# A hybrid encoder layer in float32: x normalised and split once more during the token-major projection, all neighbourhood-attention weights turned by VectorE and DMA, and attention values moved half a step on

## The chip, the cores and the metric

The kernel runs on one core of a Trainium2 chip. The metric is the device time of one execution in microseconds (us). Engines are named as the profile names them: PE is TensorE (matmuls), PEld its weight loads, DVE VectorE, ACT ScalarE, POOL GpSimd, SP the queue from which most DMAs are issued. Three timed runs of the kernel before gave 872.6 to 873.25 us, median 873.25.

## The reference

One layer over 512 tokens with 1024 channels, all float32. `h` is the RMS norm of `x`, and one wide projection feeds everything:

```python
h = rms_norm(x, mix_norm_g[l])
proj = h @ w_in[l]
ml_q, ml_k, ml_v, ml_o, ml_gates, na_qkv, xa_q, merge_pre = jnp.split(proj, split_points, axis=-1)
y_ml = mlstm_branch(ml_q, ml_k, ml_v, ml_o, ml_gates, ...)        # bidirectional, 4 heads of 128
y_na = neighbourhood_attention(na_q, na_k, na_v, na_rpb[l])       # 8 heads of 64, 8 x 64 token grid
y_xa = memory_cross_attention(xa_q, mem_k, mem_v)                 # 4 heads of 128, 256 memory tokens
gates = jax.nn.sigmoid((merge_pre + b_merge_gate[l]).astype(F32)).astype(x.dtype)
merged = g_ml * (y_ml @ w_br_ml[l]) + g_na * (y_na @ w_br_na[l]) + g_xa * (y_xa @ w_br_xa[l])
x = x + merged @ w_out[l]
x = x + conv_glu_ffn(rms_norm(x, ffn_norm_g[l]), w_ffn_up[l], ...)
return rms_norm(x, final_norm_g)
```

The norm scales each token by one number, so it can be applied to `x` before a projection or to the projection's result after it. In the neighbourhood attention each query attends to a window of 8 rows by 16 columns; the softmax weights are then multiplied with the values, for which they must lie with the keys on the partitions, that is, transposed.

## The kernel before, in words

**Precision.** PE multiplies in a reduced float32 format, so each float32 operand is split into a high and a low part, and each product is three matmuls (`mm3`, lines 222, 223, 224: high x high, high x low, low x high). Weights arrive by DMA in blocks of mostly 512 KB (`emit_raw`), up to three blocks ahead, and each is split one block ahead of its use: an ACT copy makes the high part (line 204), a VectorE subtraction the low part (line 205).

**Stages.** `XH`, `XL` are the split of x times its gain, but not yet times the norm of each token. With them run the projections of mLSTM q and k (`mlq`, `mlk`); the *token-major part* (`TMW`, blocks `tm`, three groups of columns in eight weight blocks), in which x is the stationary operand and tokens come out on partitions, for the mLSTM and neighbourhood values; then, channels on partitions again, `xaq`, `o`, memory keys and values, `naq`, `nak`; and three branches (`br` 0 to 2), each with eight gate projections (`g`) and four blocks of branch projection (`br`), followed by the output projection and the FFN. Every projection on `XH`, `XL` comes out of PSUM through a product with the token's norm: `rc` per partition in the token-major part, `rb` along the row elsewhere (VectorE, lines 1037, 1045, 1081, 1086 and, for the gates, 1109; the gates and `o` then go through a tanh on ACT).

**The attentions beside it.** The mixers (`ml_all`, `xa_all`, `na_all`) are generators. The projections call `step` or `half` in their midst, and each call runs the current generator up to its next `yield`, so that attention instructions are interleaved with projections; a gate projection drives two half steps of the neighbourhood attention, and a branch projection of one output tile one. The place of an instruction in its engine's queue then comes from the framework's own scheduling of what the generators emit. `drain` runs what is left before a branch projection reads its mixer's output.

**Neighbourhood attention.** 16 tiles (4 head pairs x 2 heads x 2 halves). In step t `scores` makes four matmuls (lines 817, 818) and the softmax of tile t. Then the weights must be turned. Tiles below `TN` = 8: `transposes`, four PE transposes into PSUM (line 836), split from there (lines 843, 844). Tiles from 8: `turn_out`, a VectorE transpose of 32 x 32 blocks (line 142) and four strided DMAs to DRAM (`td`, line 145), one step later `turn_in`, one DMA back (line 151), and `parts`, the split (lines 854, 855). `values` multiplies (line 866), `store` collects heads and splits the result (lines 882 to 889). For tiles from 8 the values stand in the second half of step t + 2. The values' right operand is loaded by 32 small POOL DMAs for each head pair (`load_vwin`, line 497).

**Memory attention.** `xa_all` works head by head with the same turning; its values stood one yield after the split of its weights.

Of the kernel before, what the change touches and what calls it, by code (L numbers as in the profile page):

```python
# [17 lines left out]
P = 128  # L18
S = 512
# [8 lines left out]
NU = 14  # L28
EB = 6
WARM = 15  # L30
TN = 8
RM, RB = 0.65, 1.3
EPS = 1e-6
NEG = -1e30
# [69 lines left out]
def hybrid_block(ctx, tc, xT, memT, wflat, vecs, gbias, nabias, outa, outb):  # L104
# [14 lines left out]
    def nm(s):  # L119
        uid[0] += 1  # L120
        return f"{s}_{uid[0]}"
# [13 lines left out]
    def atps():  # L135
        return atp.tile([P, 512], F32, tag="at", name=nm("at"))
# [17 lines left out]
    def by4(a):  # L154
        return a.rearrange("p (s b) -> p s b", s=4)
# [301 lines left out]
    def to_nav(c, t, src):  # L457
# [319 lines left out]
    def na_all(nq, nk, vw0, yh, yl):  # L777
# [52 lines left out]
                A.activation(smv[:, j, :], smv[:, j, :], AF.Copy, scale=su[:, j:j + 1])  # L830
            return sm

        def transposes(i, sm):
            pt = atps()
            for j in range(4):
                PE.transpose(pt[:, j * P:(j + 1) * P], sm[:, j * P:(j + 1) * P], ident)  # L836

            pp = []
            for bl in range(2):
                w = tp.tile([P, 4, P], F32R, tag="E", name=nm("w"), bufs=EB).rearrange("p a b -> p (a b)")  # L840
                wv = w.rearrange("p (k x q) -> p k x q", k=2, x=2)
                src = pt[:, bl * 256:(bl + 1) * 256].rearrange("p (k q) -> p k q", k=2)
                A.activation(wv[:, :, 0, :], src, AF.Copy)
                V.tensor_tensor(wv[:, :, 1, :], src, wv[:, :, 0, :].bitcast(F32), op=ALU.subtract)
                pp.append(w)
            return pp

        def parts(u):
            pp = []
            for bl in range(2):  # L850
# [40 lines left out]
        n = 16  # L891
        ops = prep(0)
        bt = bias_tile(0)
        sms, ds, us, pts = {}, {}, {}, {}
        vws = {0: vw0}

        def out(i):
            if i % 4 == 0 and i + 4 < n:
                vws[i // 4 + 1] = load_vwin(i // 4 + 1)
            store(i, values(i, pts.pop(i), vws[i // 4]))  # L900

        yield
        yield
        for t in range(n + 2):
            if t < n:
                nb = bias_tile(t + 1) if t + 1 < n else None
                sms[t] = scores(t, ops, bt)
                bt = nb
                if t % 4 == 3 and t + 1 < n:
                    ops = prep((t + 1) // 4)  # L910
            if t - 2 in us:
                pts[t - 2] = parts(us.pop(t - 2))
            elif t - 2 in pts:
                out(t - 2)
            if t - 1 in ds:
                us[t - 1] = turn_in(ds.pop(t - 1), "E", EB)
            yield
            if t - 1 in sms:
                pts[t - 1] = transposes(t - 1, sms.pop(t - 1))
            if TN <= t < n:  # L920
                ds[t] = turn_out(by4(sms.pop(t)))
            if t - 2 >= TN:
                out(t - 2)
            yield


    def xa_all(xq, mk, mv, yh, yl):
# [53 lines left out]

        q, k = prep(0)
        yield
        yield
        u = None
        for h in range(5):
            if u:
                pT = parts(u)
            if h < 4:
                sm = [scores(tq, q, k) for tq in range(2)]  # L990
            yield
            if u:
                values(h - 1, v, pT)
            if h == 4:
                break
            ds = [turn_out(by4(x)) for x in sm]
            yield
            u = [turn_in(d, "E", EB) for d in ds]
            yield
            v = prep_v(h)  # L1000
            if h < 3:
                q, k = prep(h + 1)
            yield
        yield


    gens = []
# [25 lines left out]

    xq = unit()
    for f in range(4):
        ps = proj(("xaq", f), XH, XL, at=mid())
        V.tensor_tensor(xq[:, f * S:(f + 1) * S], ps, rb, op=ALU.mult)
        mem_part(f)
        step(RB / 2)
    for f in range(4):  # L1040
        if f == 2:
            mp = rstd_parts(macc, M)
        ps = proj(("o", f), XH, XL, at=mid({4: lambda: norm.append(rstd_cols(mp, M, "m"))} if f == 3 else {}))
        t = scr()
# [4 lines left out]
        A.activation(g.rearrange("p (i s a) -> p s i a", i=4, s=4), t.rearrange("p (s i a) -> p s i a", s=4, i=4),  # L1049
                     AF.Tanh, scale=0.5)  # L1050
        V.tensor_scalar(g, g, 1.0, None, op0=ALU.add)
        step(RB / 2)
# [24 lines left out]
    nq, nk = unit(), unit()  # L1077
    rv = lambda a: a.rearrange("p (r b c) -> p b r c", r=ROWS, b=4)
    for f in range(4):
        ps = proj(("naq", f), XH, XL, at=mid())  # L1080
        V.tensor_tensor(nq[:, f * S:(f + 1) * S].rearrange("p (b r c) -> p b r c", r=ROWS, b=4), rv(ps), rv(rb),
                        op=ALU.mult)
        step(RB / 2)
    for f in range(4):
        ps = proj(("nak", f), XH, XL, at=mid())
        V.scalar_tensor_tensor(nk[:, f * S:(f + 1) * S], ps, 0.125, rb, op0=ALU.mult, op1=ALU.mult)
        step(RB / 2)

    mg = []
# [8 lines left out]
    for br in range(3):  # L1098
# [6 lines left out]
            ys[2] = [unit(F32R), unit(F32R)]  # L1105
            gens.append(na_all(nq, nk, vw0, *ys[2]))
        def gate(f, t):
            ps = proj(("g", br, f), XH, XL, at={3: half, KT - 1: half})
            V.tensor_tensor(t, ps, rb, op=ALU.mult)
# [329 lines left out]
```

## Time and profile before

| what | value |
|---|---|
| timed runs (3) | 872.6 to 873.25 us, median 873.25 |
| the profiled execution's own time | 872.36 us |
| its span, first to last instruction | 870.6 us |
| mean granted TensorE clock | 0.998 |
| DMA issues of weight turning before (all uses) | 112 writes `td<-s`, 28 reads `U<-td` |
| gate products with the norm (line 1109) | 24, 0.68 us each |

In the page, section 1 gives busy time and its share of the span, section 4 the chain of work that ended last. Groups of instructions read: line, engine, operation, output<-input, shape, count, then busy time and mean ns, then idle time ahead of them and who ended it. In a timeline the columns are start, duration, engine, line, operation. Bars on PE overlap, since a matmul's duration includes the pipeline behind it: how much of PE a matmul takes is read from the distance between starts.

### The profile page before, as it was taken

How to read it: one execution, taken by the hardware profiler on the slowest of the kernel's cores; microseconds unless marked ns; L12 is line 12 of the kernel's file. 1: busy time of each engine (PE TensorE's matmuls, PEld its weight loads, DVE VectorE, ACT ScalarE, POOL GpSimd, SP SyncE). 2: the span in 40 equal slices, each digit the busy share in tenths (PEclk: the TensorE clock that was granted, in tenths of full speed). 3: DMA queues.
4: the chain of work that ended last, by engine and by line, in shares of the span. 5: the costliest groups of instructions: out<-in, count | busy, mean ns of one | idle time of the engine just before them, and what ended most of it. 6: DMA issues, size and time to landing. Idle time of an engine off the chain costs nothing.

```text
span 870.6 us, 12197 instructions
## 1 busy us (share of the span) xinstructions
PE 862.5 (99%) x4214; PEld 727.2 (84%) x4214; DVE 596.1 (68%) x1200; ACT 447.6 (51%) x937; POOL 137.4 (16%) x218
## 2 busy tenths in 40 slices
PE   9999999999999999999999999999999999999997
PEld 7898889988888888888888888888888888888896
DVE  7696688876568768898676568777633466667443
ACT  7464457764355657787634445444422344444442
POOL 1001100000104810751001112111100011111010
PEclk9999999999999999999999999999999999999999
DMA  8235654642445733576523332223223322322443
GB/s 276 97 100 157 183 177 139 195 133 97 133 140 151 226 113 119 152 203 218 182 91 107 129 118 88 97 98 106 86 85 114 110 99 95 102 94 74 142 119 110
DMA packets 59598, 114.37 MB, mean 131 GB/s; under 512 B 8200, under 2 KB 30216, under 8 KB 59536
## 3 DMA queue, kind: packets, MB, share of 16 engines
q1 hardware_dynamic: 51888, 107.14, 38.0%
q0 software_dynamic: 7360, 6.32, 3.4%
q8 instruction: 33, 0.54, 0.3%
q14 instruction: 29, 0.24, 0.1%
q10 hardware_dynamic: 288, 0.14, 0.1%
HBM read 102.01 MB, written 11.55 MB: 130 GB/s over the span
## 4 chain that ended last, share of the span: by engine, by line
PE 98%; issue 0%; DMA 0%; DVE 0%; ACT 0%; POOLq 0%; POOL 0%; DVEq 0%; ACTq 0%
PE mm L223 29%; PE mm L222 29%; PE mm L224 29%; PE at L222 2%; PE at L223 2%; PE at L224 2%; PE at L866 1%; PE at L684 1%; PE at L686 1%; PE at L668 1%; PE at L817 0%; PE at L818 0%; PE at L628 0%; PE at L836 0%; DMA vec<-vecs 0%
## 5 line engine op out<-in xcount | busy, mean ns | idle before, releaser
L222 PE MATMUL mm<-u,w 128*128 128x512 f32 (+1 forms) x1077 | 416.4, 387 | 0.1
L223 PE MATMUL mm<-u,w 128*128 128x512 f32 (+1 forms) x1077 | 413.8, 384 | 0.3 <-DVE u L229 0.3
L224 PE MATMUL mm<-u,w 128*128 128x512 f32 (+1 forms) x1077 | 414.0, 384 | 0.0
L204 ACT ACTIVATE w<-wr 128x512 fp32r<-128x512 f32 (+1 forms) x298 | 184.6, 622 | 207.7 <-PE mm L224 171.6
L205 DVE TENSOR_TENSOR w<-wr,w 128x512 fp32r<-128x512 f32 (+3 forms) x299 | 208.2, 699 | 89.0 <-ACT w L204 86.5
L224 PEld LDWEIGHTS mm<-u,w 128*128 128x128 f32 x1077 | 202.3, 188 | 41.1 <-DVE w L205 0.6
L222 PEld LDWEIGHTS mm<-u,w 128*128 128x128 f32 x1077 | 202.5, 188 | 38.8 <-ACT u L228 0.4
L223 PEld LDWEIGHTS mm<-u,w 128*128 128x128 f32 x1077 | 202.5, 188 | 38.7 <-DVE u L229 0.6
L497 POOL DMA_DIRECT2D u<-nav_d x128 | 62.6, 516 | 97.6 <-PE at L866 50.9
L1309 POOL TENSOR_TENSOR s<-s,rb 128x512 f32<-128x512 f32 x22 | 37.3, 1697 | 248.6 <-DVE s L1308 240.6
L228 ACT ACTIVATE u<-s 128x512 fp32r<-128x512 f32 x22 | 13.9, 632 | 56.2 <-DVE s L1312 56.2
L1312 DVE TENSOR_TENSOR s<-mm,s 128x512 f32<-128x512 f32 x22 | 15.2, 690 | 22.5 <-POOL s L1309 22.5
L409 ACT ACTIVATE s<-pad,vec 128x512 f32<-128x512 f32 x30 | 24.4, 813 | 8.6 <-DVE pad L407 8.1
L410 DVE SCALAR_TENSOR_TENSOR s<-pad,vec,s 128x512 f32<-128x512 f32 x30 | 23.5, 783 | 4.6 <-ACT s L409 4.6
L1159 POOL TENSOR_TENSOR acc<-acc,s 128x512 f32<-128x512 f32 x7 | 9.0, 1289 | 102.8 <-ACT s L1158 102.8
L229 DVE SCALAR_TENSOR_TENSOR u<-s,u 128x512 fp32r<-128x512 f32 x22 | 15.2, 691 | 14.0 <-ACT u L228 14.0
L1308 DVE SCALAR_TENSOR_TENSOR s<-s,s 128x512 f32<-128x512 f32 x22 | 15.2, 692 | 13.4 <-ACT s L1307 13.3
L411 DVE SCALAR_TENSOR_TENSOR s<-pad,vec,s 128x512 f32<-128x512 f32 x30 | 22.5, 750 | 0.8
L1307 ACT ACTIVATE s<-s 128x512 f32<-128x512 f32 x22 | 13.9, 632 | 16.1 <-DVE s L1306 16.0
L827 ACT ACTIVATE s<-s,y 128x256 f32<-128x256 f32 x32 | 16.0, 501 | 7.2 <-DVE y L824 7.1
L222 PE MATMUL mm<-w,u 128*128 128x512 f32 x48 | 18.9, 393 | 0.0
L223 PE MATMUL mm<-w,u 128*128 128x512 f32 x48 | 18.7, 390 | 0.0
(294 smaller groups left out, 1001.1 us busy)
## 6 DMA issues: line engine op xcount, KB each, us to landing
wr<-wflat SPq DMA_DIRECT2D x140, 512.0 KB, 3.3
td<-s SPq DMA_DIRECT2D x112, 64.0 KB, 1.9
U<-td SPq DMA_DIRECT2D x28, 256.0 KB, 3.5
s<-xT SPq DMA_DIRECT2D x16, 256.0 KB, 4.3
nab<-nabias SPq DMA_DIRECT2D x16, 256.0 KB, 3.2
u<-nav_d POOLq DMA_DIRECT2D x128, 32.0 KB, 3.2
wr<-wflat SPq DMA_DIRECT2D x15, 192.0 KB, 2.4
nav_d<-nv POOLq DMA_DIRECT2D x8, 256.0 KB, 3.3
```

The source lines that it names most:

```text
L204: A.activation(h[:, u:v], src, AF.Copy)
L205: V.tensor_tensor(l[:, u:v], src, h[:, u:v].bitcast(F32), op=ALU.subtract)
L222: PE.matmul(ps, lh, rh, start=start, stop=False)
L223: PE.matmul(ps, lh, rl, start=False, stop=False)
L224: st["mm"] = PE.matmul(ps, ll, rh, start=False, stop=stop).ins
L229: V.scalar_tensor_tensor(l, src, scale, h.bitcast(F32), op0=ALU.mult, op1=ALU.subtract)
L409: A.activation(t1, pad[:, 0:512], AF.Identity, scale=vcol(w, i), bias=vcol(b, i))
L410: V.scalar_tensor_tensor(t1, pad[:, 1:513], vcol(w, n + i), t1, op0=ALU.mult, op1=ALU.add)
L411: V.scalar_tensor_tensor(t1, pad[:, 2:514], vcol(w, 2 * n + i), t1, op0=ALU.mult, op1=ALU.add)
L497: G.dma_start(vw[r * 32:(r + 1) * 32, i * 256:(i + 1) * 256], nav_v[hf, r, CW[b]:CW[b] + 32, hp * 256:(hp + 1) * 256])
L827: A.activation(smv[:, j, :], smv[:, j, :], AF.Exp, bias=mx[:, j:j + 1], accum_out=su[:, j:j + 1])
L1309: G.tensor_tensor(c, c, rb2, op=ALU.mult)
```

## The change

Four things, in one diff.

1. During the token-major part, x is loaded a second time, slice by slice (`xn_load`, eight DMAs on SP), multiplied by gain and norm (VectorE), and split into `NH`, `NL` (ACT copy, VectorE subtraction), one slice with each of the eight weight blocks (`xn_part`). Four buffers `xn` hold it; the four of `XH`, `XL` are not read after this part.
2. `xaq`, `o`, `naq`, `nak` and the gates project from `NH`, `NL`. Their products with `rb` go: 24 for the gates and 16 others. The tanh of `o` and of the gates reads PSUM directly; `xaq`, `naq`, `nak` are ACT copies.
3. `transposes` and `TN` go; all 16 tiles are turned by `turn_out` and `turn_in`.
4. Values stand in the first half of step t + 3 of the neighbourhood attention, and one yield later in the memory attention, where a yield at the start and one at the end go.

```diff
+    xn = [unit(F32R) for _ in range(4)]
+    NH = [xn[k // 4][:, (k % 4) * S:(k % 4 + 1) * S] for k in range(KT)]
+    NL = [xn[2 + k // 4][:, (k % 4) * S:(k % 4 + 1) * S] for k in range(KT)]
+    xs = []
+    def xn_load():
+        xs.append(scr())
+        SY.dma_start(xs[-1], xT[:, len(xs) - 1, :])
+    def xn_part(k):
+        V.scalar_tensor_tensor(xs[k], xs[k], vcol("mix_g", k), rb, op0=ALU.mult, op1=ALU.mult)
+        A.activation(NH[k], xs[k], AF.Copy)
+        V.tensor_tensor(NL[k], xs[k], NH[k].bitcast(F32), op=ALU.subtract)
+    xn_load()
     for c, n in enumerate(TMW):
...
             ws = weights(("tm", c, h))
+            if len(xs) < KT:
+                xn_load()
+            xn_part(2 * c + h if c < 2 else 6 + h)
...
-        for t in range(n + 2):
+        for t in range(n + 3):
             if t < n:
...
-                sms[t] = scores(t, ops, bt)
+                sm = scores(t, ops, bt)
...
+            if t - 3 in pts:
+                out(t - 3)
             if t - 2 in us:
                 pts[t - 2] = parts(us.pop(t - 2))
-            elif t - 2 in pts:
-                out(t - 2)
             if t - 1 in ds:
                 us[t - 1] = turn_in(ds.pop(t - 1), "E", EB)
             yield
-            if t - 1 in sms:
-                pts[t - 1] = transposes(t - 1, sms.pop(t - 1))
-            if TN <= t < n:
-                ds[t] = turn_out(by4(sms.pop(t)))
-            if t - 2 >= TN:
-                out(t - 2)
-            yield
+            if t < n:
+                ds[t] = turn_out(by4(sm))
+            if t < n + 2:
+                yield
...
-        ps = proj(("xaq", f), XH, XL, at=mid())
-        V.tensor_tensor(xq[:, f * S:(f + 1) * S], ps, rb, op=ALU.mult)
+        ps = proj(("xaq", f), NH, NL, at=mid())
+        A.activation(xq[:, f * S:(f + 1) * S], ps, AF.Copy)
...
-            ps = proj(("g", br, f), XH, XL, at={3: half, KT - 1: half})
-            V.tensor_tensor(t, ps, rb, op=ALU.mult)
-            A.activation(t, t, AF.Tanh, scale=0.5, bias=mgbh[:, gi * 8 + f:gi * 8 + f + 1])
+            ps = proj(("g", br, f), NH, NL, at={3: half, KT - 1: half})
+            A.activation(t, ps, AF.Tanh, scale=0.5, bias=mgbh[:, gi * 8 + f:gi * 8 + f + 1])
```

How this moves PE in the neighbourhood attention, second branch. Before, a stretch of one step (`KS`, `QS`, `QZ` are the operands of scores, `w` against `u` the weights and values, `ident` the identity of a transpose; twelve projection matmuls stand at each "..."):

```order
L817 MATMUL at_3711<-KS_3640,QS_3639 128x256
L818 MATMUL at_3711<-KS_3640,QZ_3335 128x256
L817 MATMUL at_3711<-KS_3640,QS_3639 128x256
L818 MATMUL at_3711<-KS_3640,QZ_3335 128x256
L866 MATMUL at_3727<-w_3678,u_3276 128x256 x2
L866 MATMUL at_3727<-w_3681,u_3276 128x256 x2
...
L836 MATMUL at_3750<-ident,s_3624 128x128 x4
...
L817 MATMUL at_3785<-KS_3640,QS_3639 128x256
```

After, the same place (24 projection matmuls stand at the "..."; its lines are numbered in the changed file, where scores are 835 and 836 and values 869):

```order
L835 MATMUL at_3894<-KS_3639,QS_3638 128x256
L836 MATMUL at_3894<-KS_3639,QZ_3364 128x256
L835 MATMUL at_3894<-KS_3639,QS_3638 128x256
L836 MATMUL at_3894<-KS_3639,QZ_3364 128x256
L869 MATMUL at_3910<-w_3842,u_3304 128x256 x2
L869 MATMUL at_3910<-w_3845,u_3304 128x256 x2
...
L835 MATMUL at_3973<-KS_3639,QS_3638 128x256
```

The set of transposes in the middle of the step is gone, and the values stand right behind the scores of a tile three steps further on.

How it moves VectorE in the token-major part, between the gates of the mLSTM (`lf`) and the last group of columns. Before (`w` from `wr` is the low part of a weight block, `wr_750` the last block of the second group, `wr_782` the first of the third, `nv` the values' eviction):

```order
L528 SCALAR_TENSOR_TENSOR lf<-y_1096,y_1105 128x32
L205 TENSOR_TENSOR w_816<-wr_750,w_816 128x512
L205 TENSOR_TENSOR w_819<-wr_750,w_819 128x512
L205 TENSOR_TENSOR w_848<-wr_782,w_848 128x512
L205 TENSOR_TENSOR w_851<-wr_782,w_851 128x512
L464 SCALAR_TENSOR_TENSOR nv_879<-mm_746,rc_x,nv_879 128x128 x2
```

After (the same two blocks are now `wr_766` and `wr_803`; `s` is a slice of x, line 478 its product with gain and norm, line 480 the low part of its split):

```order
L204 TENSOR_TENSOR w_842<-wr_766,w_842 128x512
L204 TENSOR_TENSOR w_845<-wr_766,w_845 128x512
L480 TENSOR_TENSOR u_624<-s_626,u_622 128x512
L478 SCALAR_TENSOR_TENSOR s_640<-s_640,vec,rb_x 128x512
L478 SCALAR_TENSOR_TENSOR s_701<-s_701,vec,rb_x 128x512
L480 TENSOR_TENSOR u_624<-s_640,u_622 128x512
L478 SCALAR_TENSOR_TENSOR s_774<-s_774,vec,rb_x 128x512
L480 TENSOR_TENSOR u_624<-s_701,u_622 128x512
L478 SCALAR_TENSOR_TENSOR s_811<-s_811,vec,rb_x 128x512
L480 TENSOR_TENSOR u_624<-s_774,u_622 128x512
L204 TENSOR_TENSOR w_879<-wr_803,w_879 128x512
L480 TENSOR_TENSOR u_625<-s_811,u_623 128x512
```

Eight operations on slices of x have moved in between the two weight blocks, and one more before the first of them; each waits for its slice's DMA.

More of the change, by code (lines that the diff above doesn't have):

```diff
@@ L831, in scores @@
             return sm
[L833 to L846, printed above, removed]
         def parts(u):
@@ L893, in na_all @@
         bt = bias_tile(0)
-        sms, ds, us, pts = {}, {}, {}, {}
+        ds, us, pts = {}, {}, {}
         vws = {0: vw0}
@@ L983, in xa_all @@
         yield
-        yield
-        u = None
+        pT = u = None
         for h in range(5):
@@ L991, in xa_all @@
             yield
-            if u:
+            if h < 4:
+                ds = [turn_out(by4(x)) for x in sm]
+            yield
+            if pT:
                 values(h - 1, v, pT)
[L994 to L1004, printed above, removed]
+            if h < 4:
+                u = [turn_in(d, "E", EB) for d in ds]
+                yield
+                v = prep_v(h)
+                if h < 3:
+                    q, k = prep(h + 1)
+                yield
     gens = []
@@ L1042, in hybrid_block @@
             mp = rstd_parts(macc, M)
-        ps = proj(("o", f), XH, XL, at=mid({4: lambda: norm.append(rstd_cols(mp, M, "m"))} if f == 3 else {}))
-        t = scr()
-        V.tensor_tensor(t, ps, rb, op=ALU.mult)
+        ps = proj(("o", f), NH, NL, at=mid({4: lambda: norm.append(rstd_cols(mp, M, "m"))} if f == 3 else {}))
         if f == 0:
@@ L1079, in hybrid_block @@
     for f in range(4):
[L1080 to L1082 removed]
+        ps = proj(("naq", f), NH, NL, at=mid())
+        A.activation(nq[:, f * S:(f + 1) * S].rearrange("p (b r c) -> p b r c", r=ROWS, b=4), rv(ps), AF.Copy)
         step(RB / 2)
     for f in range(4):
[L1085 to L1086 removed]
+        ps = proj(("nak", f), NH, NL, at=mid())
+        A.activation(nk[:, f * S:(f + 1) * S], ps, AF.Copy, scale=0.125)
         step(RB / 2)
```

4 lines of the change are left out of this document (1 added, 3 removed).

## The prediction

> **What bounds the kernel now.** I read the page first: busy times and the chain that ended last.
>
> ```profile
> span 870.6 us, 12197 instructions
> PE 862.5 (99%) x4214; PEld 727.2 (84%) x4214; DVE 596.1 (68%) x1200; ACT 447.6 (51%) x937; POOL 137.4 (16%) x218
> PE 98%; issue 0%; DMA 0%; DVE 0%; ACT 0%; POOLq 0%; POOL 0%; DVEq 0%; ACTq 0%
> ```
>
> TensorE (PE) is busy for 862.5 of 870.6 us, and 98% of the chain is its own stream of matmuls. So an edit is worth what it takes out of that stream, or out of the waits in it; work taken from VectorE (DVE) or ScalarE (ACT) is worth nothing by itself. Next I asked who waits for whom. The only wait of PE in the attention stage that this view names is this (waiter, releaser, total us, times, longest):
>
> ```profile
> PE at L866 <- PE mm L224: 0.2, 1, 0.2
> ```
>
> That is not all of it. Matmuls are pipelined and the drawn bars overlap, so a late start hides under the bar before it. The timeline of PE shows it in its first column, the starts. First, a set of four weight transposes (L836) among projection matmuls (L222 to L224):
>
> ```profile
> 322.26 0.39 PE L223 MATMUL mm<-u,w 128*128 128x512 f32 x1
> 322.49 0.39 PE L224 MATMUL mm<-u,w 128*128 128x512 f32 x1
> 322.72 0.60 PE L836 MATMUL at<-ident,s 128*128 128x128 f32 x4
> 323.07 0.48 PE L222 MATMUL mm<-u,w 128*128 128x512 f32 x1
> 323.39 0.39 PE L223 MATMUL mm<-u,w 128*128 128x512 f32 x1
> L836 PE MATMUL at<-ident,s x32: 270/272/273, 322.7 to 371.7; 128*128 128x128 f32 x32
> ```
>
> Projection matmuls start 0.23 us apart (322.26 to 322.49). From 322.49 to 323.39 there are two such steps, 0.46, and the set; the set costs 0.90 - 0.46 = 0.44 us. Second, the value matmuls of the attention (L866), four to a tile: one tile that was in time, then three that were not.
>
> ```profile
> 398.20 0.39 PE L224 MATMUL mm<-u,w 128*128 128x512 f32 x1
> 398.43 0.64 PE L866 MATMUL at<-w,u 128*128 128x256 f32 x4
> 398.90 0.40 PE L222 MATMUL mm<-u,w 128*128 128x512 f32 x1
> ...
> 384.00 0.39 PE L224 MATMUL mm<-u,w 128*128 128x512 f32 x1
> 384.40 1.06 PE L866 MATMUL at<-w,u 128*128 128x256 f32 x4
> 385.30 0.39 PE L222 MATMUL mm<-u,w 128*128 128x512 f32 x1
> ...
> 392.43 0.39 PE L224 MATMUL mm<-u,w 128*128 128x512 f32 x1
> 393.03 0.68 PE L866 MATMUL at<-w,u 128*128 128x256 f32 x2 [0.22 <-PE mm L224]
> 393.55 0.40 PE L222 MATMUL mm<-u,w 128*128 128x512 f32 x1
> ...
> 411.09 0.39 PE L224 MATMUL mm<-u,w 128*128 128x512 f32 x1
> 411.55 1.05 PE L866 MATMUL at<-w,u 128*128 128x256 f32 x4
> 412.44 0.40 PE L222 MATMUL mm<-u,w 128*128 128x512 f32 x1
> ```
>
> In time, a set takes 398.90 - 398.20 - 0.23 = 0.47 us. The tile at 384 takes 1.30 from matmul to matmul instead of 0.70, so 0.60 was waited; the one at 411 takes 1.35, so 0.65. At 393 only half of a set stands between, which should take 0.23 + 0.23, and takes 1.12: 0.65 again. Together 1.9 us, all in the tiles whose weights already go through VectorE and DMA. Last, how full the other engines are there (columns: stretch, length, then busy time of PE, PEld, DVE, ACT, POOL with counts, clock, DMA share, GB/s):
>
> ```profile
> 72.00:95.00 23.00, 23.00 (x147) 20.95 (x146) 9.86 (x25) 9.81 (x20) 3.79 (x8) 1.00 0.54 164
> 319.00:381.00 62.00, 62.00 (x319) 52.27 (x318) 52.12 (x135) 49.12 (x119) 20.34 (x42) 1.00 0.49 145
> 381.00:395.00 14.00, 13.76 (x65) 10.88 (x64) 13.18 (x33) 11.29 (x27) 10.33 (x22) 1.00 0.85 233
> 395.00:431.00 36.00, 35.93 (x175) 29.73 (x174) 26.67 (x71) 24.40 (x60) 0.49 (x1) 1.00 0.62 195
> ```
>
> VectorE is 84% busy while tiles 0 to 7 are transposed on PE (319 to 381), and 94% in the 14 us (381 to 395) in which turned tiles meet the merging of the second branch; two of the three late sets lie there.
>
> **The change, part by part.** *Transposes off PE.* Tiles 0 to 7 lose one set each: 8 x 0.44 = 3.5 us out of the stream. I take starts and not durations: 32 x 0.272 = 8.7 us would count each bar in full, though four of them fit between 322.72 and 323.07. The Trainium skill (TensorE: Matmul & The Clock Gate, Part 4: PE-mode transpose) puts a 128x128 bf16 transpose inside a kernel at about 275 ns. The 272 ns of the row agrees as a duration; priced by it the transposes would be worth 8.8 us and the sum below would be 862.1, which the starts speak against.
>
> *Their VectorE and DMA path.* Each of the eight tiles gains a block transpose on VectorE, four writes to DRAM and one read back; the splitting that followed the PE transpose stays, with another source.
>
> ```profile
> L142 DVE STREAM_TRANSPOSE s<-s 128x512 f32<-128x512 f32 x16 | 11.3, 706 | 1.7 <-ACT s L830 1.5
> L1109 DVE TENSOR_TENSOR s<-mm,rb_x 128x512 f32<-128x512 f32 x16 | 10.9, 680 | 5.2 <-PE mm L224 5.1
> td<-s SPq DMA_DIRECT2D x112, 64.0 KB, 1.9
> U<-td SPq DMA_DIRECT2D x28, 256.0 KB, 3.5
> s<-xT SPq DMA_DIRECT2D x16, 256.0 KB, 4.3
> ```
>
> (Groups: line, engine, tiles, count, busy us, mean ns; DMA issues: count, KB each, median us to landing.) On VectorE that is 0.71 us per tile; against it stands the multiplication by the norm in each gate (0.68), which goes. In 319 to 381 nine tiles are scored and two of those are turned already, so seven block transposes come (5.0) and the five gate products in it go (3.4): 52.1 + 1.6 = 53.7 us of VectorE work, in 62 - 3.5 = 58.5 us of PE work. That is 92% instead of 84%: between the second and third row of the table, and nearer to the crowded one. This is the unknown of the case. If nothing comes of it the price is 0. If the whole stretch behaves like 381 to 395, where 0.60 + 0.65 us were waited in 14, it is 1.25 x (58.5 + 14)/14 = 6.5 us. A gain is excluded, since nothing is in this place to be gained but what the next part counts. I take 0.6, one such wait, since the next part gives each tile more time than those had.
>
> *Values half a step on.* A tile's values came two and a half steps after its scores when turned; now it is three. Half a step is twelve projection matmuls and an attention set, 12 x 0.23 + 0.47 = 3.2 us, and no set was more than 0.65 late. So the 1.9 us go. Next in line there is the matmul stream itself, since the scores, which now stand just ahead of the values, are released by operands prepared a step before. In the memory attention the same happens between two projections:
>
> ```profile
> 277.06 0.39 PE L224 MATMUL mm<-u,w 128*128 128x512 f32 x1
> 277.39 0.50 PE L222 MATMUL at<-U,X 128*128 128x512 f32 x1
> 277.73 0.40 PE L222 MATMUL mm<-u,w 128*128 128x512 f32 x1
> ```
>
> 0.67 instead of 0.46: 0.2 us, which go too. At the far end the last tile moves half a step toward the branch projection that reads it. Its chain was:
>
> ```profile
> 430.52 0.64 PE L866 MATMUL at<-w,u 128*128 128x256 f32 x4
> 433.75 0.69 DVE L889 TENSOR_TENSOR u<-acc_y,u 128x512 fp32r<-128x512 f32 x1 [0.70 <-ACT u L888]
> ```
>
> So 434.44 - 430.52 = 3.9 us from first value matmul to last split. In the new order 21 projection matmuls stand between the set and the first matmul that reads it: 0.47 + 21 x 0.23 = 5.3 us. It is covered by 1.4 us; without that cover it would cost what it is late, once.
>
> *x scaled and split in the token-major part.* Eight loads of x on SP's queue, and per slice two VectorE operations and an ACT copy. PE needs the result only at the projection after this part. What can cost is the queueing: SP, VectorE and ACT do these ahead of weight blocks.
>
> ```profile
> 73.17 1.38 DVE L205 TENSOR_TENSOR w<-wr,w 128x512 fp32r<-128x512 f32 x2 [0.65 <-ACT w L204]
> 78.56 1.37 DVE L205 TENSOR_TENSOR w<-wr,w 128x512 fp32r<-128x512 f32 x2 [4.01 <-ACT w L204]
> ...
> 83.81 0.28 PE L222 MATMUL at<-w,u 128*128 128x256 f32 x1
> ```
>
> The block split at 78.56 is first read by PE at 83.81; it is ready at 79.93, 3.9 us early. At 0.69 per operation eight slices are 16 x 0.69 = 11.0 us of VectorE, which in 72 to 95 has 23 - 9.86 = 13.1 free; nine of the operations stand ahead of this block in the order, 6.2 us from 74.55, so it would begin at 80.8, and its first half be ready by 81.5: 2.3 us to spare, if x has come by then (4.3 us after issue, five loads together). Cost 0; bounds 0 and, were each of the three last blocks late by as much as it is early now, 3 x 3.9 = 11.7. I take 0, as no row shows PE waiting for a split in this part.
>
> *Evictions.* 40 products with the norm leave VectorE; twelve of them become ACT copies out of PSUM, the other 28 were followed by an ACT step that now reads PSUM itself. None is on PE's path: 0 on either side.
>
> **The sum.** The profiled execution took 872.36 us (span 870.6 and 1.8 around it). 872.36 - 3.5 - 1.9 - 0.2 + 0.6 = 867.4. The three timed runs before have a median of 873.25 and a lowest of 872.6, so that the profiled one is 0.9 under the median; I go half of that up, to 867.8.
>
> **The rivals.** (1) *The waits come back.* VectorE at 92%, in order, makes weights or splits late here and there: 2 to 6.5 us of new waits, 868.8 to 873.3. For it: 94% went with late sets. Against it: in those 14 us only the values were late, never a weight block, and they now have 3.2 us more. 23%.
>
> (2) *The turn is too slow, and the kernel slower.* Four strided writes, a read and a block transpose for each of 16 tiles miss even the third step, each tile waiting as the three late ones did: 16 x 0.63 = 10.1 us, 872.36 - 3.5 - 1.9 - 0.2 + 10.1 = 876.9. It decides from the point where weights come over 3.2 us later than today's turned ones. For it: the DMA share was 0.85 in the crowded stretch. Against it: of the eight turned tiles most were in time with half a step less. 5%. The Trainium skill (VectorE: DVE Perf Modes, Rules for kernel authors) speaks for this rival: a 128x128 transpose belongs on TensorE where PSUM will do as its destination, as it did here. The trace goes against it so far: the set at 398.43 came by the other path and in time.
>
> (3) *x in the way.* A weight block in the token-major part is split late, since VectorE stands in front of an x slice that has not landed: 1 to 4 us, once, 868.4 to 871.4. It decides from 2.3 us of extra lateness. 8%.
>
> (4) *The transposes cost nothing.* They filled time in which PE would have waited anyway for attention, so that only 1.9 + 0.2 - 0.6 = 1.5 us come: 870.9. Against it: the matmuls on either side of 322.72 run at the plain 0.23. 4%.
>
> **Numbers.** The forecast itself has 60%: 865.8 (no new wait, and about a us more of short late starts of the kind shown, not quoted) to 869.3. The range runs to 871.4, which takes in rival 3 and two thirds of rival 1. A measurement tells some 0.2% from no change, 1.75 us: faster is below 871.5. Faster: 0.60, 0.15 of rival 1 and 0.07 of rival 3, 0.82. Same: 0.07 of rival 1, 0.01 of rival 3, 0.04 of rival 4, 0.12. Slower: rival 2 and 0.01 of rival 1, 0.06.
>
> **What would show it.** In the profile after: no transposing matmuls in the attention stage; every value set 0.47 us by its starts, right behind its scores; projections 0.23 apart from 72 to 100; VectorE over 90% busy in the second branch. Wrong: late sets of values or scores in that branch (rival 1, or 2 if in nearly every tile); a gap ahead of a token-major block (3); a projection spacing that widened as the sets left (4).

## The result and the profile after

The changed kernel took 866.42 us (median of four runs, 866.21 to 867.39) and the kernel before 872.92 (four runs, 872.47 to 873.25): a ratio of 0.9928, 95% interval 0.9911 to 0.9945. That is 6.5 us less, where the forecast was 867.8 with a range of 865.8 to 871.4. The profiled executions differ by 872.36 - 866.28 = 6.1 us.

The page of the changed kernel begins so: span, busy time by engine, and the shares of the chain that ended last.

```profile
span 864.5 us, 12250 instructions
PE 857.0 (99%) x4182; PEld 724.5 (84%) x4182; DVE 583.1 (67%) x1184; ACT 454.8 (53%) x957; POOL 138.3 (16%) x218
PE 94%; DMA 3%; DVE 1%; issue 1%; SPq 0%; ACT 0%; POOLq 0%; POOL 0%; DVEq 0%; ACTq 0%
```

It is still a kernel bound by TensorE: 32 matmuls fewer, and busy for all but 7.5 us of the span. Where the 6 us went is to be read from PE's starts again. First a set of scores (L835; the rows show the first of the four) and values (L869) in the second branch of the changed kernel:

```profile
331.24 0.39 PE L223 MATMUL mm<-u,w 128*128 128x512 f32 x1
331.47 0.28 PE L835 MATMUL at<-KS,QS 128*128 128x256 f32 x1
...
331.94 0.64 PE L869 MATMUL at<-w,u 128*128 128x256 f32 x4
332.42 0.39 PE L221 MATMUL mm<-u,w 128*128 128x512 f32 x1
```

From the projection matmul ahead to the one behind are 332.42 - 331.24 = 1.18 us: 0.23 for the first, 0.47 for four scores, 0.48 for four values. Nothing was waited. I measured every set of the memory and the neighbourhood attention so, by its distance of starts less the median steps that its matmuls take in all traces here, and added up what was over. This *late total* is 3.0 us in the kernel before (the prediction quoted 1.9 + 0.2 of it) and 0.8 after. The only set of the neighbourhood attention that is left late:

```profile
382.68 0.39 PE L223 MATMUL mm<-u,w 128*128 128x512 f32 x1
382.91 0.28 PE L835 MATMUL at<-KS,QS 128*128 128x256 f32 x1
...
383.38 0.92 PE L869 MATMUL at<-w,u 128*128 128x256 f32 x4
384.14 0.40 PE L221 MATMUL mm<-u,w 128*128 128x512 f32 x1
```

It spans 384.14 - 382.68 = 1.46 instead of 1.18, so it was late by 0.28 us. The largest of all is in the memory attention:

```profile
301.27 0.39 PE L222 MATMUL mm<-u,w 128*128 128x512 f32 x1
301.73 0.50 PE L221 MATMUL at<-U,X 128*128 128x512 f32 x1
302.07 0.40 PE L223 MATMUL mm<-u,w 128*128 128x512 f32 x1
```

0.80 instead of the 0.46 of two plain starts: 0.34. Last the windows of the changed kernel that answer to those shown of before (stretch, length, busy PE, PEld, DVE, ACT, POOL, clock, DMA share, GB/s):

```profile
72.00:95.00 23.00, 23.00 (x146) 20.89 (x146) 19.75 (x41) 13.66 (x27) 4.71 (x8) 1.00 0.79 255
318.00:378.00 60.00, 60.00 (x299) 50.90 (x298) 53.67 (x140) 50.00 (x121) 15.66 (x33) 1.00 0.73 216
378.00:391.00 13.00, 13.00 (x65) 10.99 (x64) 12.46 (x33) 11.50 (x28) 10.54 (x22) 1.00 0.82 226
```

VectorE is busy for 53.67 of 60 us, 89%, in the branch that lost its transposes, and for 96% in the crowded stretch behind it. The matmul stream runs through both: PE has no idle time that the windows show.

### The profile page after: what moved, and what is told of

The parts are those of the page before. It is cut to its first block, busy times and chain, and to the rows that moved or that the text cites. A ratio compares the mean times of both kernels' runs of the same rounds, so it can differ in the third digit from the quotient of the medians.

```text
span 864.5 us, 12250 instructions
## 1 busy us (share of the span) xinstructions
PE 857.0 (99%) x4182; PEld 724.5 (84%) x4182; DVE 583.1 (67%) x1184; ACT 454.8 (53%) x957; POOL 138.3 (16%) x218
## 4 chain that ended last, share of the span: by engine, by line
PE 94%; DMA 3%; DVE 1%; issue 1%; SPq 0%; ACT 0%; POOLq 0%; POOL 0%; DVEq 0%; ACTq 0%
PE mm L223 28%; PE mm L221 28%; PE mm L222 28%; PE at L221 2%; PE at L222 2%; PE at L223 2%; PE at L869 1%; DMA U<-td 1%; DMA td<-s 1%; PE at L702 1%; PE at L704 1%; PE at L686 1%; DMA s<-xT 1%; DMA wr<-wflat 0%; PE at L835 0%
## 5 line engine op out<-in xcount | busy, mean ns | idle before, releaser
L204 DVE TENSOR_TENSOR w<-wr,w 128x512 fp32r<-128x512 f32 (+3 forms) x299 | 204.3, 687 | 112.2 <-ACT w L203 110.2
L141 DVE STREAM_TRANSPOSE s<-s 128x512 f32<-128x512 f32 x24 | 16.9, 708 | 3.0 <-ACT s L848 2.3
L221 PE MATMUL mm<-w,u 128*128 128x512 f32 x48 | 18.9, 393 | 0.0
```

What stands on the lines that cost most here:

```text
L141: V.transpose(t.rearrange("p (j s a) -> p s j a", j=4, s=4), src.rearrange("p s (j b) -> p s j b", j=4))
L204: V.tensor_tensor(l[:, u:v], src, h[:, u:v].bitcast(F32), op=ALU.subtract)
L221: PE.matmul(ps, lh, rh, start=start, stop=False)
```

## The experiments

The change has three parts that can be made alone: *rescale* (x normalised and split again, projections from `NH`, `NL`, products with `rb` gone), *turn* (all 16 tiles by VectorE and DMA), *half step* (values half a step on, in both attentions). The prediction's theory is this: the gain is the transposes at their price by starts, 3.5 us, and the late sets that the half step removes, with rescale worth nothing. A rival (by durations): the transposes are worth their durations, up to 8.7 us, and new waits give part back. Another (relief): rescale's relief of VectorE is what lets the turned tiles be in time. The first expectations call the prediction's theory 1 and relief 2; their 3 is that turning is simply cheap and the other parts do nothing. All eight combinations were run, and probes beside them. The table holds every kernel; the kernel before was 872.8 to 872.95 us in these comparisons.

| kernel | parts | median, us (range, runs) | ratio, 95% interval | late total, us |
|---|---|---|---|---|
| before | none | 872.9 | 1 | 3.0 |
| rescale_only | R | 871.61 (871.41 to 872.32, 11) | 0.9987, 0.9979 to 0.9996 | 2.4 |
| turn_only | T | 871.08 (870.68 to 872.06, 11) | 0.998, 0.9972 to 0.9989 | 5.2 |
| half_step_only | H | 869.79 (869.31 to 871.35, 5) | 0.9967, 0.9955 to 0.998 | 2.0 |
| rescale_and_turn | R, T | 871.33 (870.94 to 872.01, 11) | 0.9983, 0.9974 to 0.9992 | 5.2 |
| rescale_and_half_step | R, H | 869.72 (869.49 to 870.59, 5) | 0.9964, 0.9952 to 0.9977 | 0.2 |
| turn_and_half_step | T, H | 868.73 (867.65 to 868.98, 5) | 0.9948, 0.9935 to 0.996 | 2.3 |
| changed kernel | R, T, H | 866.42 (866.21 to 867.39, 4) | 0.9928, 0.9911 to 0.9945 | 0.8 |
| idle_transposes | R, T, H + 32 transposes | 870.13 (869.55 to 870.61, 5) | 0.9968, 0.9956 to 0.9981 | 0.1 |
| gate_load | R, T, H + 16 gate products | 869.34 (867.36 to 869.64, 5) | 0.9954, 0.9941 to 0.9966 | 3.6 |
| memory_values_back | R, T, H but memory attention | 866.53 (866.35 to 866.91, 5) | 0.9928, 0.9914 to 0.9941 | 0.8 |
| x_unused | T, H + x split again | 868.03 (867.1 to 868.45, 5) | 0.9943, 0.9931 to 0.9956 | 2.5 |
| turn_and_full_step | T, values a full step on | 867.09 (866.63 to 867.8, 5) | 0.9937, 0.9924 to 0.9951 | 0.4 |
| changed_full_step | R, T, values a full step on | 866.12 (865.82 to 866.27, 5) | 0.9923, 0.991 to 0.9935 | 0.5 |

The late total is of the one profiled execution, which lies up to 1.6 us from its kernel's median. The counts that the expectations quote (5.3, 5.7, 0.9) are higher by up to 0.5. One line fits the table: 865.5 us, plus the late total, plus 3.9 where PE transposes eight tiles, within 0.8 us of each profiled execution's own time. The 865.5 is fitted to these runs; the 3.9 is measured below (idle_transposes). Part of what is left is the start of an execution: its sixty-first projection matmul starts between 19.48 us (before) and 20.18 (x_unused), long before the kernels differ on PE.

### turn_only

```diff
-TN = 8
+TN = 0
```

> The kernel before with all 16 tiles turned by VectorE and DMA, nothing else: gate products stay, values of turned tiles two and a half steps after their scores. Theory 1: 3.5 us of transposes go, but VectorE has 52.1 + 5.0 = 57.1 us of work in 58.5 and most sets come late, 2 to 8 us: 870 to 877, with late sets in the trace for more than half of the tiles. Theory 2: VectorE gets more work and PE was never the limit there: slower by 1 us or more. Theory 3 (turning is simply cheap; the other two parts do nothing): 869 to 869.5, late sets no more than the three or four before.

Measured 871.08, 1.8 us less than before, not 3.5. The late total rises by 2.2, from 3.0 to 5.2. PE of turn_only at one of the late tiles (in this kernel L817 and L866 are scores and values):

```profile
338.61 0.39 PE L224 MATMUL mm<-u,w 128*128 128x512 f32 x1
339.32 1.03 PE L866 MATMUL at<-w,u 128*128 128x256 f32 x4 [0.32 <-DVE w L855]
340.18 0.28 PE L817 MATMUL at<-KS,QS 128*128 128x256 f32 x1
```

The values took 340.18 - 338.61 - 0.23 = 1.34 us instead of 0.47. VectorE of the same kernel at that time shows who held them up:

```profile
338.24 0.71 DVE L142 STREAM_TRANSPOSE s<-s 128x512 f32<-128x512 f32 x1 [1.42 <-ACT s L830]
338.88 0.72 DVE L855 TENSOR_TENSOR w<-U,w 128x256 fp32r<-128x256 f32 x2
```

VectorE stood idle for 1.42 us in front of the block transpose of a later tile, whose softmax ACT had not finished. The split of the tile that PE needed (L855, the low parts) is queued behind it. On ACT the high parts of the same split stood behind that softmax too:

```profile
338.12 0.71 ACT L854 ACTIVATE w<-U 128x256 fp32r<-128x256 f32 x2
```

So the order on both engines made this tile late. The window of turn_only's branch:

```profile
318.00:378.00 60.00, 59.39 (x285) 49.11 (x284) 53.68 (x138) 47.42 (x113) 15.51 (x32) 1.00 0.68 199
```

VectorE is as busy as in the changed kernel (53.68 and 53.67 us). What is wrong at this tile is the order: work for a later tile stands in front of the split that PE needs next, and two and a half steps between scores and values don't cover that.

### half_step_only

```diff
-        for t in range(n + 2):
+        for t in range(n + 3):
...
+            if t - 3 in pts:
+                out(t - 3)
             if t - 2 in us:
                 pts[t - 2] = parts(us.pop(t - 2))
-            elif t - 2 in pts:
-                out(t - 2)
...
-            if t - 2 >= TN:
-                out(t - 2)
-            yield
+            if t < n + 2:
+                yield
```

The memory attention is as in the changed kernel. For tiles 0 to 7, whose values stood in the first half of step t + 2, the edit is a full step, in the changed kernel too.

> The kernel before with only the values moved on (first half of step t + 3 for all tiles, one yield in the memory attention). Theory 1: the late sets go and nothing else, 1.9 to 2.6 us: 870.3 to 871. Theory 2 and 3: no change, 872.5 to 873.2.

Measured 869.79, 3.1 us less and more than the 1.9 to 2.6 expected. That is as much as the whole late total of the kernel before, and in the neighbourhood attention of the profiled execution no late set is left. The profile of this kernel fell on the slowest of its five executions (871.35), and there two sets of the memory attention waited 1.95 us. PE's row for one of them, from that profile:

```profile
289.61 0.50 PE L222 MATMUL at<-U,X 128*128 128x512 f32 x1 [0.82 <-ACT U L969]
```

ACT's row there, the split ahead of it, names a DMA read:

```profile
289.14 0.72 ACT L969 ACTIVATE U<-U 128x256 fp32r<-128x256 f32 x2 [1.37 <-DMA U<-td]
```

So the memory attention can lose about 2 us to a late read in a single execution, which the median doesn't show.

### rescale_only and rescale_and_turn

rescale_only is points 1 and 2 of the change in the kernel before, all else as it was; rescale_and_turn adds `TN = 0`. The edit in its core:

```diff
+            xn_part(2 * c + h if c < 2 else 6 + h)
...
-            ps = proj(("g", br, f), XH, XL, at={3: half, KT - 1: half})
-            V.tensor_tensor(t, ps, rb, op=ALU.mult)
-            A.activation(t, t, AF.Tanh, scale=0.5, bias=mgbh[:, gi * 8 + f:gi * 8 + f + 1])
+            ps = proj(("g", br, f), NH, NL, at={3: half, KT - 1: half})
+            A.activation(t, ps, AF.Tanh, scale=0.5, bias=mgbh[:, gi * 8 + f:gi * 8 + f + 1])
```

> The kernel before with only x's second, scaled split and the projections from it; weights turned as before (eight tiles on PE), values where they were. Theory 1 (the gain is what leaves PE's stream: 3.5 us of transposes and some 2 us of late value sets): the transposes stay and the late sets at most shrink, so 0 to 1 us faster than the 872.9 before, 872 to 873. Theory 2 (the relief of VectorE is what pays, 24 gate products and 16 others less): most of the 6.5 us, 867 to 869.

> The changed kernel without the half step: x scaled and split again, all 16 tiles turned, values two and a half steps after the scores. Theory 1: the transposes are gone, the late sets stay in some tiles (three of eight before, so some six of sixteen at 0.6): 868.5 to 871. Theory 2 and 3: as the changed kernel, 866 to 867.

Rescale alone takes off 1.2 us, with an interval of 0.4 to 1.8 us: small, but not nothing, and more than the 0 to 1 expected. Its late total falls by 0.6. Its profiled execution took 872.24, hardly less than that of before, but lost 0.5 us at its start (sixty-first projection matmul at 19.98 instead of 19.48). The other 0.6 us of the median are not placed. Together with turn it takes off 1.5, no more than turn by itself and less than expected: without the half step the late total stays at 5.2. PE of rescale_and_turn at one tile, half a set between two projection matmuls:

```profile
335.81 0.39 PE L222 MATMUL mm<-u,w 128*128 128x512 f32 x1
336.48 0.56 PE L885 MATMUL at<-w,u 128*128 128x256 f32 x2 [0.28 <-DVE w L874]
336.88 0.40 PE L223 MATMUL mm<-u,w 128*128 128x512 f32 x1
```

1.07 us instead of 0.23 + 0.23: late by 0.61, for a split on VectorE (L874 is `parts` here). The split itself waited for ACT, whose high part (L873) ended at 335.97, behind the softmax of a later tile:

```profile
335.57 0.40 ACT L873 ACTIVATE w<-U 128x256 fp32r<-128x256 f32 x1
336.00 0.43 DVE L874 TENSOR_TENSOR w<-U,w 128x256 fp32r<-128x256 f32 x1
```

A freer VectorE doesn't mend that. It has more room in this kernel than in turn_only: it is busy for 51.38 of the 60 us from 318, against 53.68. So the theory of relief falls as it stands: relief without the half step brings nothing to the turned tiles.

### rescale_and_half_step, and idle_transposes

rescale_and_half_step is the changed kernel with `TN = 8` and `transposes` kept. idle_transposes is the changed kernel with eight sets of four PE transposes of the identity put back in the steps where they stood, into a PSUM tile that nothing reads; their waits and their splits aren't put back.

```diff
             yield
+            if 1 <= t <= 8:
+                pt = atps()
+                for j in range(4):
+                    PE.transpose(pt[:, j * P:(j + 1) * P], ident, ident)
```

> The changed kernel with its first eight tiles transposed on PE as before. All theories of the stream: the changed kernel plus eight sets at 0.44 us, 866.4 + 3.5 = 869.9, about the half step alone (869.8). If the turning pays in another way than by what leaves PE: nearer to 868 or to 871.5.

> The changed kernel with eight sets of four PE transposes put back that serve nothing: they transpose the identity into a PSUM tile that nobody reads, one set in the middle of each of the steps 1 to 8. It prices the sets alone, without their splits and without the tiles' dependence on them. By the starts: 8 x 0.44 = 3.5 us, 866.4 + 3.5 = 869.9. By the durations: 8.7 us, 875.1. If the sets filled time in which PE would wait anyway: 866.4.

With rescale and half step in place, turning all tiles is worth 869.72 - 866.42 = 3.3 us. Putting bare transposes back costs 870.13 - 866.42 = 3.7. Both lie near the price by starts (3.5) and far from the 8.7 by durations. PE of idle_transposes (L924 the transposes):

```profile
335.58 0.39 PE L223 MATMUL mm<-u,w 128*128 128x512 f32 x1
335.81 0.60 PE L924 MATMUL at<-ident 128*128 128x128 f32 x4
336.17 0.48 PE L221 MATMUL mm<-u,w 128*128 128x512 f32 x1
336.48 0.39 PE L222 MATMUL mm<-u,w 128*128 128x512 f32 x1
```

336.48 - 335.58 - 0.46 = 0.44 us a set again, while its group has 271 ns for one:

```profile
L924 PE MATMUL at<-ident 128*128 128x128 f32 x32 | 4.8, 271 | 0.0
```

The theory by durations falls with that. The whole stretch gives the price without waits. These are the same two projection matmuls, 200 apart, first in the changed kernel, then in idle_transposes; no set between them is late in either:

```profile
320.98 0.39 PE L222 MATMUL mm<-u,w 128*128 128x512 f32 x1
373.75 0.39 PE L221 MATMUL mm<-u,w 128*128 128x512 f32 x1
```

```profile
320.66 0.39 PE L222 MATMUL mm<-u,w 128*128 128x512 f32 x1
377.29 0.39 PE L221 MATMUL mm<-u,w 128*128 128x512 f32 x1
```

56.63 - 52.77 = 3.86 us for eight sets, 0.48 each. rescale_and_half_step and half_step_only take 56.63 there too. The 0.44 looks at a set's neighbours alone; where the stretch has 0.04 more for each set is open.

### turn_and_half_step, x_unused and gate_load

turn_and_half_step is the changed kernel without rescale: the projections use `XH`, `XL` and the products with `rb` are back. x_unused adds to it only the loads, products and splits of x in the token-major part, which nothing reads. gate_load puts only the 16 gate products of the second and third branch back into the changed kernel, behind the tanh and into a tile that nobody reads, so that VectorE has the work and nobody waits for its result (the PSUM tile is held until it has been read):

```diff
             A.activation(t, ps, AF.Tanh, scale=0.5, bias=mgbh[:, gi * 8 + f:gi * 8 + f + 1])
+            if br:
+                V.tensor_tensor(pads[f % 2][:, 1:513], ps, rb, op=ALU.mult)
```

> The changed kernel without its rescaling: projections from x unscaled, each followed by its product with the norm on VectorE; all 16 tiles turned, values half a step on. In the kernels so far, late sets were 3.0 us before, 5.3 with the turning alone, 5.7 with turning and rescaling. Theory 1 as first stated (rescaling makes the room on VectorE without which the turning stalls): 57.1 us of VectorE work in 58.5, so 2 to 5 us of late sets or late weight blocks, 868 to 871. Theory 3, as it stands now (turning pays only with the half step, and the rescaling is a side matter): within 0.7 us of the changed kernel, 866 to 867.2.

> Turning and half step (868.7), and x loaded, scaled and split a second time in the token-major part, but nobody reads it: the projections stay on the unscaled x with their products. It prices what the second split itself costs, DMAs and SP's queue included. As predicted for that part, 0: 868.3 to 869.1. If slices of x hold up weight blocks: 869.5 to 872.

> The changed kernel with the 16 gate products of the second and third branch put back on VectorE; their results go into a spare tile that nobody reads, and the tanh still reads PSUM. It adds 16 x 0.68 = 11 us of VectorE work beside the neighbourhood attention and nothing to any chain but the release of a PSUM bank. If the rescaling is worth its 2.3 us (868.7 without it, 866.4 with it) because it clears VectorE there: 868 to 869, late sets of 2 us or more. If what counts is the shorter chain of a gate or the other 24 products: 866.2 to 867.

Without rescale the time is 868.73, 2.3 us over the changed kernel. The split of x itself costs nothing that can be told (868.03 against 868.73, ranges overlapping). The 16 products alone cost 2.9 by the medians, in single executions 0.9 to 3.2. The late total rises by 2.8 with them, from 0.8 to 3.6, which is nearly all of it, so the PSUM tile that is held longer adds nothing that can be seen. So what rescale brings is VectorE time beside the neighbourhood attention, and it is the work and not the wait of a consumer that counts. PE of gate_load where it lost most:

```profile
357.26 0.39 PE L223 MATMUL mm<-u,w 128*128 128x512 f32 x1
...
357.84 0.28 PE L836 MATMUL at<-KS,QZ 128*128 128x256 f32 x1
359.14 1.05 PE L869 MATMUL at<-w,u 128*128 128x256 f32 x4 [1.01 <-PE at L836]
360.03 0.40 PE L221 MATMUL mm<-u,w 128*128 128x512 f32 x1
```

From 357.26 to 360.03 are 2.77 us instead of 1.18. The row names L836, which had long ended: what the values need is the split of their weights on VectorE. VectorE of gate_load had fallen behind one tile earlier; L840 takes the scores out of PSUM, L1106 is the product that was put back, L858 the split that PE waits for:

```profile
353.48 0.69 DVE L1106 TENSOR_TENSOR pad<-mm,rb_x 128x512 f32<-128x512 f32 x1
354.09 0.41 DVE L840 CUSTOM_DVE_ANT_0 s<-at,nab 128x256 f32<-128x256 f32 x1
...
358.02 0.71 DVE L141 STREAM_TRANSPOSE s<-s 128x512 f32<-128x512 f32 x1
358.65 0.72 DVE L858 TENSOR_TENSOR w<-U,w 128x256 fp32r<-128x256 f32 x2
```

The same place in the changed kernel:

```profile
351.43 0.42 DVE L840 CUSTOM_DVE_ANT_0 s<-at,nab 128x256 f32<-128x256 f32 x1 [0.23 <-PE at L836]
...
355.38 0.71 DVE L141 STREAM_TRANSPOSE s<-s 128x512 f32<-128x512 f32 x1
356.01 0.72 DVE L858 TENSOR_TENSOR w<-U,w 128x256 fp32r<-128x256 f32 x2
```

In the changed kernel VectorE waits for these scores (0.23 us idle) and takes them at 351.43. In gate_load it comes to them at 354.09, with no idle time ahead, and the whole chain behind, up to the split (358.65 instead of 356.01), is 2.6 us late. The late work is passed on: softmax, turn and split all hang on the scores. The average of the stretch doesn't show this. gate_load's window, which answers to 53.67 us of VectorE in the changed kernel:

```profile
318.00:378.00 60.00, 58.80 (x287) 49.40 (x286) 54.28 (x139) 47.35 (x118) 15.52 (x32) 1.00 0.73 211
```

54.28 us, 1% more of the stretch, though PE stood idle for 1.2 us in it.

### turn_and_full_step, changed_full_step and memory_values_back

Two kernels move the values another half step on, to the second half of step t + 3 (turn_and_half_step and the changed kernel, with the same edit), and the neighbourhood attention has one yield less at its start. One kernel is the changed one with the memory attention's order as before.

```diff
         yield
-        yield
         for t in range(n + 3):
...
-            if t - 3 in pts:
-                out(t - 3)
...
             if t < n:
                 ds[t] = turn_out(by4(sm))
-            if t < n + 2:
-                yield
+            if t - 3 in pts:
+                out(t - 3)
+            yield
```

> Turning and half step without the rescaling (868.7), with the values of the neighbourhood attention another half step on (second half of step t + 3) and one yield less at its start. If the late sets there come from weights that a crowded VectorE hands over late, 3.2 us more of time clear them: 866.2 to 867. If VectorE at its limit holds back weight blocks and scores too: still 868 or more.

> The changed kernel with the values of the neighbourhood attention another half step on, and one yield less at its start. Its trace has 0.9 us of late sets left, 0.3 of it here: 866.0 to 866.5, no change that can be told. If it is worth more, lateness is more frequent in the timed runs than in the profiled one: 865 to 865.8.

> The changed kernel with the memory attention's values and yields as before; only the neighbourhood attention has its values half a step on. Theory 1: the small waits of the memory attention come back (0.2 to 0.7 us) and nothing else, 866.6 to 867.1. Rival: its half step was worth more, or the shift of one yield in the start of the neighbourhood attention matters: 867.5 or more.

Without rescale the extra half step takes off 1.6 us (868.73 to 867.09) and the late total falls from 2.3 to 0.4. So more lead can stand in for VectorE's room. With rescale it takes off 0.3, which can't be told from nothing; 866.12 is the lowest median of all kernels here, but not a gain that the runs establish. The memory attention's half step is worth 0.1, nothing: 866.53 with it taken back.

## Why the prediction was right, step by step

**Transposes, -3.5.** Right in mechanism and nearly in size: 3.3 with everything else in place, 3.7 by putting bare ones back, 3.9 by the stretch without waits. The Trainium skill (TensorE: Matmul & The Clock Gate, Part 4: PE-mode transpose) has about 275 ns for one of 128x128 bf16 inside a kernel. The duration of the float32 ones here agrees (271 ns), but 3.86 us for 32 is 0.12 us each: here that figure is the length of a bar and not what a transpose takes out of a stream of matmuls.

**Late value sets, -1.9 and -0.2.** Right in kind, short in size: the half step alone took off 3.1 us and the late total of before is 3.0, since five smaller ones, late by 0.1 to 0.3 each, add up to 0.9 us that the prediction did not quote. The -0.2 of the memory attention was no gain: a set there still waits 0.34, in another place (301.73), and undoing the edit changes 0.1.

**New waits, +0.6.** Somewhat high: one set of the neighbourhood attention is late, by 0.28, and none in the stretch of 60 us that the prediction feared for. The upper bound, 6.5, was not idle either: turn_only holds 5.2 us of late sets. The prediction's reason, that each tile now has half a step more, is what the runs show: 5.2 (rescale_and_turn) against 0.8.

**x in the token-major part, 0.** Right. From the first matmul of this part to the first behind it, PE takes 45.3 us both before (50.06 to 95.33) and after (50.31 to 95.56), and in every other trace here. VectorE was busy for 19.75 of the 23 us from 72, against 9.86 + 11.0 = 20.9 expected. VectorE's rows of the changed kernel for the block that was in question, its two halves:

```profile
81.24 0.69 DVE L204 TENSOR_TENSOR w<-wr,w 128x512 fp32r<-128x512 f32 x1
...
82.44 0.69 DVE L204 TENSOR_TENSOR w<-wr,w 128x512 fp32r<-128x512 f32 x1
```

And PE's first read of it:

```profile
84.05 0.28 PE L221 MATMUL at<-w,u 128*128 128x256 f32 x1
```

The first half is ready at 81.93, 2.1 us before PE reads it (forecast 2.3), and the second at 83.13.

**Evictions, 0, and "work taken from VectorE is worth nothing by itself".** This is the sentence that was too strong. Alone it nearly holds (1.2 us, interval 0.4 to 1.8). With all tiles turned and the half step in place it fails: the same relief is worth 2.3 us, or 2.9 by gate_load. The sum came out since the prediction charged the crowding of VectorE with the relief already counted in (its 92%, measured 89%), but as a list of what each part is worth it had 0 where 2.3 stands.

**End of the branch.** It was covered as said. PE of the changed kernel, the last set of values:

```profile
427.19 0.64 PE L869 MATMUL at<-w,u 128*128 128x256 f32 x4
```

And VectorE's last split behind it:

```profile
430.37 0.69 DVE L892 TENSOR_TENSOR u<-acc_y,u 128x512 fp32r<-128x512 f32 x1 [0.70 <-ACT u L891]
```

431.06 - 427.19 = 3.9 us, inside the 5.3 of the matmuls between.

**The rivals.** The second rival, a turn too slow, did not come about: of the sets of 16 turned tiles one is late, by 0.28 us, although the changed kernel issues more DMAs. The DMA issues of the changed kernel (count, KB each, median us to landing):

```profile
td<-s SPq DMA_DIRECT2D x144, 64.0 KB, 2.1
U<-td SPq DMA_DIRECT2D x36, 256.0 KB, 3.5
```

2.1 us for a write instead of 1.9, and the read as it was. By the rule that a 128x128 transpose belongs on TensorE (the Trainium skill, VectorE: DVE Perf Modes, Rules for kernel authors) the changed kernel would lose; rescale_and_half_step against the changed kernel, 869.72 to 866.42, goes against it in this kernel, where PE is the bound and lead time can be had. turn_only and rescale_and_turn show where it would nearly be right: with the values half a step earlier, new waits eat most of what turning saves, and 1.8 us are left without rescale, 0.3 with it.

The first rival, waits that come back, is what turn_only and rescale_and_turn are. It needs the half step or the relief to be missing. The third (x in the way) and the fourth (transposes that cost nothing) are refuted above.

**What the sum missed.** By own times the gain is 6.1 where the sum had 5.0. The late total fell by 2.2 to 2.3 (3.0 to 0.8) where the sum had 1.5, and the transposes were 3.9 where it had 3.5; against that the profiled execution after lost 0.2 at its start (sixty-first projection matmul at 19.69 instead of 19.48). That leaves 0.1 to 0.2 unplaced. The low end of the forecast, 865.8, was given for just this case: no new wait, and more short late starts than were quoted.

## What to carry to other kernels

Price an operation in a stream by the distance of starts around it and not by its bar, and look for hidden waits the same way: sets late by 0.1 to 0.7 us each were worth 3 us that the view of waits had as 0.2. Moving work from the bounding engine onto others pays only if each result then has lead enough to sit out a queue in order: the same turn was worth 0.3 us (over rescale alone), 1.8 (over the kernel before), 1.1 (over the half step alone) or 3.3 (over both), depending on when its results were wanted and how full VectorE was. Parts of such a change don't add: VectorE relief and the move look small alone (1.2 and 1.8 us), and are worth 2.3 and 3.3 once the other parts are in.

## What the runs showed of the hardware that was not expected

Four transposes of 128x128 float32 in a stream of float32 matmuls take 0.48 us out of it, 0.12 each, where each bar is 0.27; filled with the identity (idle_transposes) or with data (rescale_and_half_step), the same. A set of values that starts late also runs slower: its four matmuls took 340.18 - 339.32 = 0.86 us in turn_only and 360.03 - 359.14 = 0.89 in gate_load, against 332.42 - 331.94 = 0.48 in time. Why is open, but a late start of 0.48 us in turn_only cost 0.86. An engine's busy share over 60 us says little about whether its results come in time: 53.68 us of VectorE in turn_only's stretch went with 5.2 us of late sets in its attentions, 53.67 in the changed kernel's with 0.8. Eight more reads of 256 KB and 32 more writes of 64 KB in the same time moved the median landing of the writes from 1.9 to 2.1 us, that of the reads not at all (3.5). Reads of the attention's bias tiles landed later, 4.0 us instead of 3.2, but 2.9 in changed_full_step, so the number of transfers alone doesn't set that.
